# Conditioning vectors formed as columns by TensorE, their bias carried with the small vectors, context blocks rounded on ScalarE

## The chip, the core and the metric

The kernel runs on one core of a Trainium2 chip. The metric is device time in microseconds of one execution, median of several. Names used below: PE is TensorE's matrix multiplication (PEld its weight loads), DVE is VectorE, ACT is ScalarE, POOL is GpSimd, SP is SyncE, whose queue carries most DMA transfers.

A matrix product on TensorE has a stationary operand (the weights, loaded by a weight load; here up to 128 columns) and a moving operand that streams through (here up to 512 columns). Operands in plain float32 are taken in two passes, so that one product in the program shows as two weight loads and two MATMUL records in the trace. Operands of type float32r take one pass. A transpose is a product with the identity.

## What is computed

One layer of a trunk over 2048 latent tokens of width 1024, with a context prefix of 256 tokens. The part of the reference that the change touches is the conditioning ("ada") of both streams, and the modulated context:

```python
ada = jnp.einsum('bd,lde->lbe', jax.nn.silu(c), w_ada) + b_ada[:, None, :]
ada_c = jnp.einsum('d,lde->le', jax.nn.silu(c_ctx), w_ada) + b_ada
...
sh1, sc1, g1, sh2, sc2, g2 = (m[:, None, :] for m in jnp.split(ada[l], 6, axis=-1))
csh1, csc1, cg1, csh2, csc2, cg2 = jnp.split(ada_c[l], 6, axis=-1)
...
hc = modulate(rmsnorm(xc, norm_mix[l]), csh1, csc1)      # h * (1 + scale) + shift
logf_f, k_f, logf_b, k_b, vc = hgrn2_gates(hc @ w_in[l][:, :3 * w], lb_f, lb_b, first)
...
h = modulate(rmsnorm(x, norm_mix[l]), sh1, sc1)
o, _, _ = token_mixers(h @ w_in[l], ...)
x = x + g1 * (o @ w_out[l])
x = x + g2 * conv_ffn(modulate(rmsnorm(x, norm_ffn[l]), sh2, sc2), ...)
```

`w_ada` is 1024 x 6144. The first stage of the kernel needs its first 2048 columns: the shift (columns 0 to 1023) and the scale (1024 to 2047), for two vectors, c and c_ctx.

## The kernel before

Activations lie transposed in SBUF, features on the 128 partitions, so shift and scale are wanted as columns: `s1` and `a1`, each 128 partitions x 2 streams x 8 blocks, where `a1` holds (1 + scale) times the gain `norm_mix`. Every large product is made of three float32r products: each operand is split into a rounded part (`hi`, a cast on ScalarE) and the rest (`lo`, a subtraction on VectorE or GpSimd), and hi x hi, lo x hi and hi x lo are added in PSUM. In the trace the context's parts are `ch` and `cl`, those of a weight tile `whi` and `wlo`.

The stage that the change edits is written in an order of its own (`manual_schedule`): each engine runs its instructions in the order of the source. The first 2048 columns of `w_ada` come as four groups g of 512 columns, each in two halves q (four of the eight 128-row blocks of the contraction). Groups 0 and 1 are the shift, 2 and 3 the scale. The work on them:

- Groups 2, 0 and 3 go through TensorE in `ada_products`: the two silu vectors `cs2` (2 columns) are the weights, and a tile of `w_ada` streams as 512 moving columns. The result is two rows of 512. `ada_columns` adds the bias row on VectorE, transposes the rows in four pieces of 2 x 128, and `put_ada` writes them to `s1` or `a1`.
- Group 1 goes through VectorE: `ada_sums` multiplies each `w_ada` block by a scalar and adds it to `acc` (16 instructions, whose start value holds the bias row), and TensorE adds `acc` over the partitions by products with a vector of ones (8 products, bank `pz`).
- The small vectors (norm gains, biases of other parts) come by ScalarE's DMA queue as rows of one tile `vr`, and one transpose makes columns of them, `vec`.
- The context's 256 rows are normalised (`x_square`, `x_scale`) and transposed into four PSUM banks `pct`. `ctx_mod` modulates one block of 128 features (VectorE, line 232), rounds it (ScalarE, line 120) and subtracts (GpSimd for blocks 0 to 3, VectorE for 4 to 7, line 121).

The tiles of `w_in` come through a ring of three SBUF buffers, `raw`; the first two hold the context's rows until these have been transposed. `split_w` makes `whi` and `wlo` of one column tile of 128, into one of two slots. After the edited stage, Tile's scheduler decides each engine's order: twelve context column tiles of 24 products each (three per head), and beside them `x_start`, which squares, scales, transposes and modulates the first eight blocks of latent rows. From there on the large products of the input projection fill TensorE.

Of the kernel before, what the change touches and what calls it, by code (L numbers as in the profile page):

```python
# [9 lines left out]
F32 = mybir.dt.float32  # L10
# [4 lines left out]
ALU = mybir.AluOpType  # L15
# [57 lines left out]
def tile_trunk(ctx, tc, x, c, cx, c_ctx, w_ada, b_ada, norm_mix, norm_ffn, w_in, hg_norm, sgu_g, sgu_b,  # L73
# [104 lines left out]
    with es1:  # L178
# [13 lines left out]
        def bank(tag):  # L192
            return ps.tile([P, 512], F32, tag=tag, name=tag, bufs={"pj": 3, "sc": 2, "mi": 3}[tag])
# [46 lines left out]

        cc = pm.tile([P, 2, 8], F32, name="cc")
# [4 lines left out]
        wts, rows, pa, nxt = {}, {}, {}, {}  # L246
# [12 lines left out]
        def load_bias(g, tag):  # L259
            rows[g] = pm.tile([2, 512], F32, tag=tag, name="rows", bufs=2)  # L260
            ld(rows[g], b_ada[0:1, g * 512:(g + 1) * 512].broadcast_to([2, 512]))

        def ada_products(g, q):
            if q == 0:
                pa[g] = bank("pj")
            for k in range(4 * q, 4 * q + 4):
                T.matmul(pa[g][:2, :], cs2[:, k, :], wts[g, q][:, k % 4, :], start=(k == 0), stop=(k == 7))

        def ada_columns(g):
            V.tensor_add(rows[g], rows[g], pa.pop(g)[:2, :])  # L270
            pv = bank("pj")
            for j in range(4):
                T.transpose(pv[:, 2 * j:2 * j + 2], rows[g][:, j * P:(j + 1) * P], ident[:2, :2])
            put_ada(g, [pv[:, w:8:2] for w in range(2)])
# [7 lines left out]
        def put_ada(g, cols):  # L282
            sl = slice(4 * (g % 2), 4 * (g % 2) + 4)
            for w in range(2):
                if g < 2:
                    V.tensor_copy(s1[:, w, sl], cols[w])
                else:
                    V.scalar_tensor_tensor(out=a1[:, w, sl], in0=cols[w], scalar=1.0, in1=nmix[:, sl],
                                           op0=ALU.add, op1=ALU.mult)
# [4 lines left out]
        def ctx_mod(k, eng):  # L294
            x_mod(pct[k // 2][:, (k % 2) * 256:(k % 2) * 256 + 256], 1, k, chl[:, k, :], cll[:, k, :], CTX, eng)
# [4 lines left out]
        with tc.manual_schedule():  # L300
# [3 lines left out]
            vr = pm.tile([50, P], F32, tag="gu", name="vr", bufs=2)  # L304
            for a, n, r0 in ((norm_mix[0], 8, 0), (norm_ffn[0], 8, 8), (hg_norm[0], 4, 16), (sgu_g[0], 4, 20),
                             (sgu_b[0], 4, 24), (conv_b[0], 22, 28)):
                S.dma_start(vr[r0:r0 + n, :], a.rearrange("(r p) -> r p", p=P))
            load_bias(2, "ot")
# [3 lines left out]
            load_bias(0, "ot")  # L312
            for w in range(2):
                ld(acc[0:1, w, :], b_ada[0:1, 512:1024])
            load_bias(3, "vv")
            load_ada(3)
            load_raw((0, CTX))
            S.activation(sg, cc, AF.Sigmoid)
# [5 lines left out]
            T.transpose(pv[:, :50], vr, ident[:50, :50])  # L324
            V.tensor_copy(vec, pv[:, :50])
            ada_products(2, 1)
            ada_columns(2)
# [7 lines left out]
            load_raw((HW, CTX))  # L335
            ada_products(0, 1)
            ada_columns(0)
            ada_sums(4, 5)
            for k in range(4):
                ctx_mod(k, G)  # L340
                if k == 1:
                    ada_sums(5, 6)
            ada_products(3, 0)
# [3 lines left out]
            ada_sums(6, 8)  # L347
            nxt[0, CTX] = split_w((0, CTX), G)
# [6 lines left out]
            ada_columns(3)  # L355
            put_ada(1, [pz[:, 8 * w:8 * w + 8:2] for w in range(2)])
            for k in range(4, NK):
                ctx_mod(k, V)
            nxt[HW, CTX] = split_w((HW, CTX), V)
# [1349 lines left out]
```

## Time and profile before

| | us |
|---|---|
| median of 3 runs | 2528.61 |
| lowest and highest | 2525.8, 2529.62 |
| the profiled execution, its own time | 2527.3 |
| its span, first to last instruction | 2525.3 |

| engine | busy us | share of the span |
|---|---|---|
| PE | 2441.6 | 97% |
| PEld | 2016.9 | 80% |
| DVE | 1798.5 | 71% |
| POOL | 1059.3 | 42% |
| ACT | 957.6 | 38% |

How the lines are read. A line of the view in order of time gives the start, the duration, the engine, the line of the source, the operation, "out<-in" by the program's names, the shape, the count of instructions merged, and in brackets the idle time of the engine before it with what ended it. A line by stretches gives the stretch, its length, and for each engine named the busy time and the count; then the granted clock of TensorE (1.00 is full, 0.50 half), the DMA share and GB/s. A line of the view by groups gives line, engine, operation, names, shapes, count, then busy us and mean ns of one, then idle us before with what ended it. The recorded end of a MATMUL is modelled, and matmuls overlap, so their price is read from start to start.

### The profile page before, as it was taken

The numbers are of one execution on the slowest core, as the hardware profiler recorded it, in microseconds if no ns is written. First come the engines' busy times: TensorE is split into PE (matmuls) and PEld (weight loads), VectorE is DVE, ScalarE is ACT, GpSimd is POOL, SyncE is SP. The second block draws the span as 40 slices with busy tenths as digits, with TensorE's granted clock in tenths as the row PEclk, the third lists the DMA queues.
The fourth block names the chain that finished last, engine by engine and source line by source line (L and its number), as shares of the span: only waits on it lengthen the run. The fifth ranks groups of instructions, "written<-read, shape, count | busy, mean of one in ns | idle before, by whom it ended". The sixth has DMA issues, their size and how long they took to land.

```text
span 2525.3 us, 32815 instructions
## 1 busy us (share of the span) xinstructions
PE 2441.6 (97%) x11859; PEld 2016.9 (80%) x11859; DVE 1798.5 (71%) x2375; ACT 957.6 (38%) x1598; POOL 1059.3 (42%) x871
## 2 busy tenths in 40 slices
PE   7999999999999999899999999999999999999998
PEld 4787887888888888788778888878878887888886
DVE  5867884745756647465699778749999993676875
ACT  3553334434334343245433333324333342332352
POOL 1444232232233343100587787877778870000002
PEclk9999999999999999999999999999999999999999
DMA  8365436563353322668932222472222248843754
GB/s 292 101 196 171 143 116 199 183 241 117 117 180 127 115 84 101 225 210 251 306 104 83 95 79 88 147 260 85 81 91 85 96 134 332 280 150 128 235 160 149
DMA packets 305838, 400.13 MB, mean 158 GB/s; under 512 B 33025, under 2 KB 216057, under 8 KB 301965
## 3 DMA queue, kind: packets, MB, share of 16 engines
q1 hardware_dynamic: 302420, 397.30, 47.5%
q8 instruction: 94, 1.54, 0.2%
q10 hardware_dynamic: 3257, 0.75, 0.1%
q14 instruction: 67, 0.55, 0.1%
HBM read 288.85 MB, written 109.13 MB: 158 GB/s over the span
## 4 chain that ended last, share of the span: by engine, by line
PE 38%; DVE 7%; DMA 3%; issue 1%; POOL 1%; ACT 0%; SPq 0%; POOLq 0%; DVEq 0%; ACTq 0%
PE up L65 26%; PE dn L65 12%; DVE dn L1297 3%; DMA mr<-m 1%; DMA sT<-wd 1%; DVE edges L1302 1%; DVE mhl L121 0%; DMA raw<-in_w_up_dram 0%; POOL Al L121 0%; DVE gp L1373 0%; DMA yl<-yd 0%; DVE mr L1552 0%; DVE odd L1577 0%; DVE odd L1643 0%; POOL cv L1384 0%
## 5 line engine op out<-in xcount | busy, mean ns | idle before, releaser
L1297 DVE SCALAR_TENSOR_TENSOR dn<-gp,taps,dn 128x1024 f32<-128x1024 f32 x352 | 448.1, 1279 | 20.6 <-ACT dn L1294 17.4
L121 POOL TENSOR_TENSOR Al<-raw,Ah 128x512 fp32r<-128x512 f32 x264 | 344.6, 1313 | 97.5 <-ACT Ah L120 89.3
L65 PE MATMUL pj<-xh,whi 128*128 128x512 f32 x896 | 364.1, 407 | 0.5 <-ACT xh L120 0.5
L65 PE MATMUL pj<-xl,whi 128*128 128x512 f32 x896 | 351.3, 392 | 1.8 <-DVE xl L121 1.1
L65 PE MATMUL pj<-xh,wlo 128*128 128x512 f32 x896 | 351.5, 392 | 1.0 <-DVE wlo L121 1.0
L65 PE MATMUL dn<-th,mhl 128*128 128x512 f32 x1120 | 347.8, 392 | 3.1 <-ACT mhl L120 1.9
L65 PE MATMUL up<-xah,Al 128*128 128x512 f32 x704 | 277.0, 393 | 2.7 <-POOL Al L121 2.7
L65 PE MATMUL up<-xah,Ah 128*128 128x512 f32 x704 | 277.6, 394 | 1.9 <-ACT Ah L120 1.9
L65 PE MATMUL up<-yl,Ah 128*128 128x512 f32 x704 | 275.0, 391 | 2.6 <-DMA yl<-yd 2.6
L120 ACT CAST Ah<-raw 128x512 fp32r<-128x512 f32 x264 | 160.4, 618 | 292.9 <-PE up L65 241.8
L65 PEld LDWEIGHTS dn<-th,mhl 128*128 128x128 f32 x1120 | 211.0, 188 | 52.4 <-ACT mhl L120 2.3
L121 POOL TENSOR_TENSOR wlo<-raw,whi 128x1024 fp32r<-128x1024 f32 x56 | 142.2, 2539 | 217.7 <-ACT whi L120 185.5
L113 POOL TENSOR_SCALAR rs<-ss 128x2 f32<-128x2 f32 (+1 forms) x16 | 7.7, 480 | 534.2 <-ACT jk L1569 363.8
L65 PE MATMUL dn<-tl,mhl 128*128 128x512 f32 x560 | 221.5, 396 | 0.0
L65 PE MATMUL up<-yh,Ah 128*128 128x512 f32 x528 | 208.3, 395 | 0.0
L65 PE MATMUL up<-yh,Al 128*128 128x512 f32 x528 | 206.9, 392 | 0.0
L65 PE MATMUL up<-xal,Ah 128*128 128x512 f32 x528 | 206.3, 391 | 0.0
L65 PEld LDWEIGHTS pj<-xh,wlo 128*128 128x128 f32 x896 | 168.4, 188 | 37.0 <-DVE wlo L121 1.7
L65 PEld LDWEIGHTS pj<-xh,whi 128*128 128x128 f32 x896 | 169.0, 189 | 34.0 <-issue 3.5
L65 PEld LDWEIGHTS pj<-xl,whi 128*128 128x128 f32 x896 | 169.1, 189 | 33.1 <-DVE xl L121 2.1
L65 PE MATMUL dn<-wo,o 128*128 128x512 f32 x768 | 185.1, 397 | 3.7 <-DMA wo<-wo_d 2.2
L65 PEld LDWEIGHTS dn<-wo,o 128*128 128x128 f32 x768 | 143.0, 190 | 34.1 <-DMA wo<-wo_d 3.0
(321 smaller groups left out, 4662.2 us busy)
## 6 DMA issues: line engine op xcount, KB each, us to landing
raw<-in_w_up_dram SPq DMA_DIRECT2D x88, 512.0 KB
mr<-m SPq DMA_DIRECT2D x85, 512.0 KB
raw<-in_w_in_dram SPq DMA_DIRECT2D x68, 512.0 KB
sT<-wd SPq DMA_DIRECT2D x88, 256.0 KB
raw<-in_w_ada_dram SPq DMA_DIRECT2D x32, 512.0 KB
m<-cv SPq DMA_DIRECT2D x22, 544.0 KB
raw<-in_w_down_dram SPq DMA_DIRECT2D x22, 512.0 KB
wd<-raw SPq DMA_DIRECT2D x22, 512.0 KB
```

Of the source, the lines that this page charges most:

```text
L65: return self.engine.matmul(out, lhsT, rhs, **kw)
L113: keep(G.tensor_scalar(out=r[:, :n], in0=ss, scalar1=scale, scalar2=bias, op0=ALU.mult, op1=ALU.add))
L120: keep(S.copy(hi, raw))
L121: (eng or G).tensor_sub(lo, raw, hi.bitcast(F32))
L1297: V.scalar_tensor_tensor(out=cr, in0=gt[:, t // 3:t // 3 + RH, t % 3:t % 3 + GW], scalar=taps[:, t * NF + f:t * NF + f + 1], in1=cr, op0=A ...
L1302: V.scalar_tensor_tensor(out=e[:, 0, :], in0=gt[:, 1, t % 3:t % 3 + GW], scalar=taps[:, t * NF + f:t * NF + f + 1], in1=e[:, 0, :], op0=AL ...
```

## The change

- The two roles of the operands are exchanged in `ada_products`: tiles of `w_ada`, 128 x 128, are the weights, and the two columns of `cs2` stream. The result lies as columns in PSUM. Each half q of a group gives its own sum: 16 products (4 pieces of 128 columns, each over 4 blocks of the contraction), where there were 4. `put_ada` adds the two halves on VectorE.
- `load_bias`, the bias rows, `ada_columns` with its twelve small transposes, and the bias rows put into `acc` go. The 2048 bias values come as 16 more rows of `vr` (one more transfer on ScalarE's queue), and after the transpose they are copied to `bc`, with 1 added for the scale.
- `put_ada` handles both streams in one instruction of 128 x 2 x 4, with the gain multiplied in one more for the scale.
- `ctx_mod` has its own code. For blocks 0 to 3 ScalarE modulates and then rounds by a copy; for blocks 4 to 7 VectorE modulates while ScalarE modulates and rounds by itself, from PSUM. The subtraction is on VectorE for blocks 0 to 3, 4 and 6, on GpSimd for 5 and 7.
- `load_raw((HW, CTX))` is called earlier in the source; its transfer still waits until the context's rows have been transposed. Both first weight tiles are split ahead of the second half of group 3, on VectorE.
- The acc sums of group 1 stand in another place: ten before the shift of group 0, six behind it.

In the changed program's order on the engines, VectorE's addition for the first half of group 3 stands behind the six sums and the four subtractions of blocks 0 to 3, and the products of the second half of group 3 on TensorE wait for that addition. ScalarE's casts for the first two weight tiles follow block 3, and the cast for the fourth tile follows three of the four squares of the latent rows. SP's transfers of the second and third weight tile wait for the transposes of the context, with the latent rows behind them, as before. From about the 390th product of TensorE on, the order on the engines is that of the kernel before.

```diff
@@ -238,12 +238,13 @@
 
 
 
         cc = pm.tile([P, 2, 8], F32, name="cc")
         ld(cc[:, 0, :], c[0].rearrange("(p k) -> p k", k=8))
         ld(cc[:, 1, :], c_ctx.rearrange("(p k) -> p k", k=8))
         sg = pm.tile([P, 2, 8], F32, name="sg")
         wv = w_ada.rearrange("(p k) e -> p k e", k=8)
-        wts, rows, pa, nxt = {}, {}, {}, {}
+        wts, pa, nxt = {}, {}, {}
         pct = [bank("mi"), bank("mi"), bank("mi"), bank("sc")]
         xc = [raw_tile() for i in range(2)]
         acc = ph.tile([P, 2, 512], F32, tag="S", name="acc")
@@ -256,22 +257,15 @@
                 wts[g, q] = t.rearrange("p a (b e) -> p (a b) e", e=512)
                 ld(wts[g, q], wv[:, 4 * q:4 * q + 4, g * 512:(g + 1) * 512])
 
-        def load_bias(g, tag):
-            rows[g] = pm.tile([2, 512], F32, tag=tag, name="rows", bufs=2)
-            ld(rows[g], b_ada[0:1, g * 512:(g + 1) * 512].broadcast_to([2, 512]))
+        bc = pm.tile([P, 16], F32, name="bc")
 
         def ada_products(g, q):
             if q == 0:
                 pa[g] = bank("pj")
-            for k in range(4 * q, 4 * q + 4):
-                T.matmul(pa[g][:2, :], cs2[:, k, :], wts[g, q][:, k % 4, :], start=(k == 0), stop=(k == 7))
-        def ada_columns(g):
-            V.tensor_add(rows[g], rows[g], pa.pop(g)[:2, :])
-            pv = bank("pj")
             for j in range(4):
-                T.transpose(pv[:, 2 * j:2 * j + 2], rows[g][:, j * P:(j + 1) * P], ident[:2, :2])
-            put_ada(g, [pv[:, w:8:2] for w in range(2)])
+                for k in range(4):
+                    T.matmul(pa[g][:, 8 * q + 2 * j:8 * q + 2 * j + 2], wts[g, q][:, k, j * P:(j + 1) * P],
+                             cs2[:, 4 * q + k, :], start=(k == 0), stop=(k == 3))
 
         def ada_sums(k0, k1):
             for k in range(k0, k1):
@@ -279,20 +273,32 @@
                     V.scalar_tensor_tensor(out=acc[:, w, :], in0=wts[1, k // 4][:, k % 4, :], scalar=cs2[:, k, w:w + 1],
                                            in1=acc[:, w, :], op0=ALU.mult, op1=ALU.add)
 
-        def put_ada(g, cols):
+        def put_ada(g, cols, q):
             sl = slice(4 * (g % 2), 4 * (g % 2) + 4)
-            for w in range(2):
-                if g < 2:
-                    V.tensor_copy(s1[:, w, sl], cols[w])
-                else:
-                    V.scalar_tensor_tensor(out=a1[:, w, sl], in0=cols[w], scalar=1.0, in1=nmix[:, sl],
-                                           op0=ALU.add, op1=ALU.mult)
+            dst = (s1, a1)[g // 2][:, :, sl]
+            V.tensor_add(dst, cols, dst if q else view(bc, 4 * g, [[0, 2], [1, 4]]))
+            if g > 1 and q:
+                V.tensor_mul(dst, dst, view(vec, sl.start, [[0, 2], [1, 4]]))
+        def ada_put(g, q):
+            put_ada(g, pa[g][:, 8 * q:8 * q + 8].rearrange("p (j w) -> p w j", w=2), q)
 
         chl = pk.tile([P, NK, CTX], F32R, tag="F", name="ch", align_bytes=AL)
         cll = ph.tile([P, NK, CTX], F32R, tag="Q", name="cl", align_bytes=AL)
 
         def ctx_mod(k, eng):
-            x_mod(pct[k // 2][:, (k % 2) * 256:(k % 2) * 256 + 256], 1, k, chl[:, k, :], cll[:, k, :], CTX, eng)
+            pt = pct[k // 2][:, (k % 2) * 256:(k % 2) * 256 + 256]
+            sc, sh = a1[:, 1, k:k + 1], s1[:, 1, k:k + 1]
+            fl = pm.tile([P, 512], F32, tag="sig", name="xfl", bufs=2)
+            if k < 4:
+                S.activation(fl[:, :CTX], pt, AF.Identity, bias=sh, scale=sc)
+                S.copy(chl[:, k, :], fl[:, :CTX])
+            else:
+                V.tensor_scalar(out=fl[:, :CTX], in0=pt, scalar1=sc, scalar2=sh, op0=ALU.mult, op1=ALU.add)
+                S.activation(chl[:, k, :], pt, AF.Identity, bias=sh, scale=sc)
+            eng.tensor_sub(cll[:, k, :], fl[:, :CTX], chl[:, k, :].bitcast(F32))
 
         xg = [ph.tile([P, D], F32, tag=t, name="xg", bufs=2) for t in ("vt", "vt", "sgt", "sgt")]
         x_rows = [x[i * P:(i + 1) * P, :] for i in range(2 * NCH)]
@@ -301,30 +307,29 @@
             load_ada(2)
             for i in range(2):
                 ld(xc[i], cx[0][i * P:(i + 1) * P, :])
-            vr = pm.tile([50, P], F32, tag="gu", name="vr", bufs=2)
-            for a, n, r0 in ((norm_mix[0], 8, 0), (norm_ffn[0], 8, 8), (hg_norm[0], 4, 16), (sgu_g[0], 4, 20),
-                             (sgu_b[0], 4, 24), (conv_b[0], 22, 28)):
+            vr = pm.tile([66, P], F32, tag="gu", name="vr", bufs=2)
+            for a, n, r0 in ((norm_mix[0], 8, 0), (b_ada[0, 0:2 * D], 16, 50), (norm_ffn[0], 8, 8), (hg_norm[0], 4, 16),
+                             (sgu_g[0], 4, 20), (sgu_b[0], 4, 24), (conv_b[0], 22, 28)):
                 S.dma_start(vr[r0:r0 + n, :], a.rearrange("(r p) -> r p", p=P))
-            load_bias(2, "ot")
             for q in range(2):
                 load_ada(0, q)
                 load_ada(1, q)
-            load_bias(0, "ot")
-            for w in range(2):
-                ld(acc[0:1, w, :], b_ada[0:1, 512:1024])
-            load_bias(3, "vv")
             load_ada(3)
             load_raw((0, CTX))
+            load_raw((HW, CTX))
             S.activation(sg, cc, AF.Sigmoid)
             V.tensor_mul(cs2.rearrange("p k w -> p w k"), cc, sg)
             ss = x_sums()
             x_square(xc, ss, keep=lambda i: i)
             ada_products(2, 0)
             pv = bank("sc")
-            T.transpose(pv[:, :50], vr, ident[:50, :50])
+            T.transpose(pv[:, :66], vr, ident[:66, :66])
             V.tensor_copy(vec, pv[:, :50])
+            V.tensor_copy(bc[:, :8], pv[:, 50:58])
+            V.tensor_scalar(out=bc[:, 8:], in0=pv[:, 58:66], scalar1=1.0, scalar2=None, op0=ALU.add)
             ada_products(2, 1)
-            ada_columns(2)
+            for q in range(2):
+                ada_put(2, q)
             x_scale(xc, ss, keep=lambda i: i)
             ada_sums(0, 4)
             ada_products(0, 0)
@@ -332,31 +337,30 @@
                 for i in range(2):
                     o = (k % 2) * 256 + i * P
                     T.transpose(pct[k // 2][:, o:o + P], xc[i][:, k * P:(k + 1) * P], ident)
-            load_raw((HW, CTX))
             ada_products(0, 1)
-            ada_columns(0)
             ada_sums(4, 5)
+            for q in range(2):
+                ada_put(0, q)
+            ada_products(3, 0)
+            ada_sums(5, 8)
             for k in range(4):
-                ctx_mod(k, G)
-                if k == 1:
-                    ada_sums(5, 6)
-            ada_products(3, 0)
+                ctx_mod(k, V)
+            ada_put(3, 0)
             load_raw((2 * HW, CTX))
             for i in range(4):
                 ld(xg[i], x_rows[i])
-            ada_sums(6, 8)
-            nxt[0, CTX] = split_w((0, CTX), G)
+            for c in (0, HW):
+                nxt[c, CTX] = split_w((c, CTX), V)
             ada_products(3, 1)
             pz = bank("pj")
             for w in range(2):
                 for j in range(4):
                     o = 2 * (4 * w + j)
                     T.matmul(pz[:, o:o + 2], acc[:, w, j * P:(j + 1) * P], ones[:, :2], start=True, stop=True)
-            ada_columns(3)
-            put_ada(1, [pz[:, 8 * w:8 * w + 8:2] for w in range(2)])
+            ada_put(3, 1)
+            put_ada(1, pz[:, :16:2].rearrange("p (w j) -> p w j", w=2), 0)
             for k in range(4, NK):
-                ctx_mod(k, V)
-            nxt[HW, CTX] = split_w((HW, CTX), V)
+                ctx_mod(k, G if k % 2 else V)
         xl = p1.tile([P, NK, TH], F32R, tag="xl", name="xl", align_bytes=AL)
         xh = p1.tile([P, NK, TH], F32R, tag="xh", name="xh", align_bytes=AL)
 
```

## The prediction

> **What bounds the kernel now.** I read the page first, then the busy time by stage, then the order of time of the first 60 us. The chain of waits is followed back only to 1229 us, so it says nothing of the stage that is edited.
>
> ```profile
> PE 2441.6 (97%) x11859; PEld 2016.9 (80%) x11859; DVE 1798.5 (71%) x2375; ACT 957.6 (38%) x1598; POOL 1059.3 (42%) x871
> ```
>
> TensorE is busy for 97% of the span: a delay of its stream comes out nearly whole at the end. The stages (us, then busy time of PE, PEld, DVE, ACT, POOL, then granted clock):
>
> ```profile
> 30.00:40.00 10.00, 6.44 (x22) 1.87 (x20) 9.83 (x12) 2.57 (x5) 6.92 (x5) 1.00 1.05 377
> 60.00:70.00 10.00, 8.78 (x70) 8.25 (x71) 10.00 (x16) 5.49 (x11) 3.86 (x2) 1.00 0.49 142
> ```
>
> Between 30 and 40 us VectorE has 9.83 of 10 us: it, not TensorE, holds back the first context product. In order of time:
>
> ```profile
> 7.09 4.89 PE L65 MATMUL pj<-wa,cs 128*2 128x512 f32 x8 [7.09 <-DMA wa<-in_w_ada_dram]
> 11.91 0.26 PE L69 MATMUL sc<-ident,vr 50*128 50x50 f32 x1
> 12.10 3.60 PE L65 MATMUL pj<-wa,cs 128*2 128x512 f32 x8
> 17.06 1.41 DVE L227 TENSOR_SCALAR raw<-raw,rs 128x1024 f32<-128x1024 f32 x2
> 20.33 1.53 PE L69 MATMUL mi<-ident,raw 128*128 128x128 f32 x12
> 21.69 0.60 PE L69 MATMUL sc<-ident,raw 128*128 128x128 f32 x4
> 22.15 5.39 DVE L279 SCALAR_TENSOR_TENSOR acc<-wa,cs,acc 128x512 f32<-128x512 f32 x8 [3.69 <-DMA acc<-in_b_ada_dram]
> 22.22 3.60 PE L65 MATMUL pj<-wa,cs 128*2 128x512 f32 x8
> 33.96 5.71 DVE L279 SCALAR_TENSOR_TENSOR acc<-wa,cs,acc 128x512 f32<-128x512 f32 x4
> 39.10 2.32 PE L65 MATMUL pj<-ones,acc 128*128 128x2 f32 x16 [3.56 <-POOL wlo L121]
> 41.87 0.58 PE L65 MATMUL pj<-ch,whi 128*128 128x256 f32 x1
> ```
>
> Each half group of conditioning is 4 products, shown as 8 passes: 3.60 us, but 4.89 for the first, where the clock was still low. The acc sums start 3.69 us late, behind a bias row's transfer, and end at 39.67; the ones products follow, and the first context product starts at 41.87. That moment is what the change moves.
>
> **The passes that replace the products.** A half group becomes 16 products of 128 weight columns on 2 moving columns: 32 passes. The ones products have exactly this shape, with both clocks in their one burst (first row: weight loads):
>
> ```profile
> 39.07:40.40 1.33, 1.33 (x12) 1.00 0.87 313
> ...
> 40.64 0.35 PE L65 MATMUL pj<-ones,acc 128*128 128x2 f32 x1
> 40.86 0.35 PE L65 MATMUL pj<-ones,acc 128*128 128x2 f32 x1
> 41.07 0.35 PE L65 MATMUL pj<-ones,acc 128*128 128x2 f32 x1
> ```
>
> At clock 1.00 a pass costs 1.33/12 = 0.111 us, at 0.50 (41.07 - 40.64)/2 = 0.215. A half group is then 3.55 or 6.88 us, where it was 3.60. So the clock decides the sign:
>
> ```profile
> 6.33:9.74 3.41, 2.65 (x4) 0.50 (x5) 0.00 (x0) 0.00 (x0) 0.00 (x0) 1.00 1.05 411
> 37.05:40.46 3.41, 1.36 (x13) 1.39 (x13) 3.21 (x3) 0.00 (x0) 1.41 (x1) 1.00 0.97 376
> 40.46:43.87 3.41, 3.41 (x19) 3.38 (x19) 1.31 (x7) 0.40 (x1) 0.00 (x0) 0.50 1.02 343
> 43.87:47.29 3.42, 3.33 (x14) 2.72 (x12) 2.24 (x6) 1.01 (x3) 0.00 (x0) 0.50 0.23 87
> ...
> 40.46:41.86 1.40, 1.40 (x10) 0.50 0.97 255
> 41.86:43.87 2.01, 2.01 (x10) 0.50 1.05 405
> ```
>
> The clock changes only at steps of 3.41 us. The stretch 6.33 to 9.74 raised it with 2.65 us of streaming (its 1.00 is filled in, as no clock change precedes it: the passes ran at half speed). The stretch 40.46 to 43.87 had TensorE busy throughout and did not raise it (it stayed 0.50 to 47.29): 1.40 us of 2-column passes and 2.01 us of 256-column products. If a stretch is judged by a sum of its work, the bar lies above 2.01 and at or below 2.65 us of streaming, and 1.40 us of 2-column work counts for less than 0.64. A stretch full of it counts for less than 3.41 x 0.64 / 1.40 = 1.56, below a bar that 2.01 missed. So in the changed kernel, which starts cold and issues only such passes, I take 0.215 for all of them; the other end is 0.111. The Trainium skill, TensorE: Matmul & The Clock Gate, Part 1, says the same of the default (half rate until a busy window of about 3.4 us) and the trace agrees at 3.41; its word is "busy", and if weight loads were busy, rival C's time would follow.
>
> **The change part by part**, against the profiled execution (2527.3 us; span 2525.3).
>
> 1. TensorE's way to the first context product. It starts at 7.09 as before (the same transfers lead). Six half groups are 192 passes, the ones products 16: 208 x 0.215 = 44.7. The 16 transposes of the context took 1.89 us to 22.22; at half clock 3.8 (the rows for either end). The transpose of the small vectors 0.3 (0.26 before). The last half group writes the bank that VectorE's addition for the half group before it reads, so TensorE waits for that addition, behind VectorE's sums and subtractions; at half clock these are done by about 45 and it is a hop of 0.2 to 0.7, I take 0.5. Sum: 7.1 + 44.7 + 3.8 + 0.3 + 0.5 = 56.4, against 41.87: **+14.5**.
>
> 2. What is removed is hidden by this. Three bias additions, twelve transposes and five bias transfers go, the acc sums lose their 3.69 us wait, and four evictions leave VectorE; but with sums ending near 43, TensorE arrives at the ones products at 53. The bias in ScalarE's transfers adds one issue and 8 KB, due at 12 to 14 us: nothing. SP's queue loses five issues, but its second and third weight blocks wait for the transposes (now about 32), and the rows of x behind them; they are needed after 60.
>
> 3. The context blocks. Prices:
>
> ```profile
> L221 ACT ACTIVATE xjk<-xg 128x1024 bf16<-128x1024 f32 x4 | 4.2, 1060 | 0.0
> L121 POOL TENSOR_TENSOR cl<-xfl,ch 128x256 fp32r<-128x256 f32 x4 | 4.2, 1058 | 17.1 <-ACT ch L120 17.1
> L121 DVE TENSOR_TENSOR cl<-xfl,ch 128x256 fp32r<-128x256 f32 x4 | 1.7, 425 | 1.9 <-ACT ch L120 1.9
> L232 DVE TENSOR_SCALAR xfl<-mi,a,s 128x256 f32<-128x256 f32 x6 | 3.1, 538 | 0.3 <-POOL cl L121 0.2
> L514 ACT ACTIVATE cS<-pj 128x256 f32<-128x256 f32 x2 | 0.8, 380 | 0.2 <-issue 0.2
> ```
>
> Blocks 0 to 3 fall under TensorE's delay. Blocks 4 to 7 need the shift, which comes after the ones products: 0.3, then on VectorE 4 x 0.54 + 2 x 0.43 = 3.0, the last subtraction on GpSimd 1.06, its products 0.4: 4.8 us for the first column tile. ScalarE's rounding from PSUM (0.38, by its 128x256 activation) runs beside. Before:
>
> ```profile
> 48.22 0.28 PE L65 MATMUL pj<-ch,wlo 128*128 128x256 f32 x1
> 57.80 0.28 PE L65 MATMUL pj<-ch,wlo 128*128 128x256 f32 x1
> 57.92 0.28 PE L65 MATMUL pj<-ch,whi 128*128 128x256 f32 x1
> ...
> 53.88 1.05 ACT L120 CAST whi<-raw 128x1024 fp32r<-128x1024 f32 x1 [1.62 <-PE pj L65]
> ...
> 48.47 1.23 DVE L121 TENSOR_TENSOR wlo<-raw,whi 128x1024 fp32r<-128x1024 f32 x1 [0.52 <-ACT whi L120]
> 51.25 1.22 DVE L121 TENSOR_TENSOR wlo<-raw,whi 128x1024 fp32r<-128x1024 f32 x1 [1.55 <-ACT whi L120]
> 54.97 1.23 DVE L121 TENSOR_TENSOR wlo<-raw,whi 128x1024 fp32r<-128x1024 f32 x1 [2.49 <-ACT whi L120]
> 59.24 1.42 DVE L227 TENSOR_SCALAR xg<-xg,rs 128x1024 f32<-128x1024 f32 x2 [0.91 <-POOL rs L115]
> ...
> 64.47 0.21 DVE L477 TENSOR_TENSOR tot<-tot 128x64 f32<-128x64 f32 x1
> 66.34 0.42 DVE L470 TENSOR_TENSOR cS<-cS,tot 128x256 f32<-128x256 f32 x1
> ```
>
> 41.87 to 48.5 was 6.6: **-1.8**.
>
> 4. The second column tile. Its weight split moves ahead; it ran from 48.5 to 53.8 (the slot that the cast at 53.88 waited for), with a wait for wlo and a low clock; with neither, 24 products at the 0.12 between the rows at 57.80 and 57.92 are 2.9: **-2.4**.
>
> 5. Given back. In the changed order ScalarE's cast for the fourth tile stands behind the second tile's first sigmoid and three squares: 0.2 + 2 x 0.3 + 2 x 1.15 after the second tile ends, then 1.05 + 1.23 + 0.2 for the split: 5.6, against 2.9 of third tile: up to 2.7 of stall, or none if TensorE fills it. I take **+1.3**. VectorE is full from 60 to 70; of its scan updates two pairs of a total and an update (0.21 + 0.42 each) move ahead of the scaling of x: **-1.3**.
>
> Sum: 14.5 - 1.8 - 2.4 + 1.3 - 1.3 = **+10.3**: 2537.6. The shown runs' median, 2528.6, is 1.3 above the profiled one: **2539 us**.
>
> **Rivals.** *B: the transposes raise the clock.* 3.8 us of 128-column streaming could lift it for one step of 3.41 us, which does 6.6 us of cold passes: 3.2 less, 2536. For: they stream; against: they straddle two stretches. The Trainium skill, same page, Part 4, says that transposes do not count as busy in the same way; by it B falls and 2539 stands; no row here decides.
>
> *C, the other side: the clock rises as it did at 9.74 and 2-column passes keep it.* Then 12 passes cold to 9.74 and 20 x 0.111 to 12.0; four half groups, 14.2, transposes 1.9, vectors 0.2: 28.3; the wait of part 1 decides now: the 16 sums at 5.39/8 = 0.67 from about 17.6 (group 2 done at 15.7, its additions 0.5, the scaling 1.41) end at 28.7 with two additions, four subtractions 1.7, and the addition: 31. Then 3.55 + 16 x 0.111: 36.4, that is -5.5, and parts 3 to 5 unchanged: -9.7, **2519**. For: before stayed at 1.00 from 9.74 to 40.46. Against: it streamed 512 columns there, and the stretch 37.05 to 40.46, with 1.36 us of 2-column passes, lost the clock.
>
> *D: the delay is swallowed.* From 48.5 to 59.24 VectorE idles 5.5 us (0.52, 1.55, 2.49 and 0.91 ahead of its splits and scaling); if the x path used that, +4.8, 2533. Against: ScalarE's squares stand behind the late sigmoids in the order.
>
> **How the numbers follow.** Forecast 0.53, B 0.23, C 0.16, D 0.08. The forecast's own range is 2535 to 2543 (stall 0 to 2.7, hop and transposes 1 each way). Leaving out C and a little of each tail: 2527 to 2545. What this kernel's runs can tell from no change is about 0.2%, 5 us: slower holds the forecast and most of B, 0.73; within, the rest of B and D, 0.11; faster C, 0.16.
>
> **What would show it.** Right: 2-column passes 0.215 apart up to about 53 us, no raised clock before the context products, the first of these near 56. B: one raised step after the transposes. C: 0.111 apart and the first context product near 36. Wrong altogether: that product near 56 and an end within 5 us of before.

## The result and the profile after

The changed kernel ran in 2547.36 us (median of four: 2547.71, 2539.53, 2547.3, 2547.41), the kernel before beside it in 2527.2: slower by a ratio of 1.0072 [1.0057, 1.0087]. The profiled execution is the one of 2547.71 us, span 2545.6: **+20.3 us** over the profiled execution of before, where the sum had +10.3. The forecast's direction was right, its size half, and the time lies above the range. A second group of runs (six of the changed kernel, the first experiment below) puts the two medians 17.3 us apart, so the 20.3 of this pair may hold some of the spread of single executions.

The page's line of engines; TensorE is again busy for 97% of a longer span:

```profile
PE 2464.9 (97%) x11991; PEld 2057.8 (81%) x11991; DVE 1799.0 (71%) x2374; ACT 959.7 (38%) x1602; POOL 1048.6 (41%) x868
```

TensorE's first 57 us in order of time (start, duration, engine, line, operation, count, idle time before and what ended it):

```profile
7.25 6.96 PE L65 MATMUL pj<-cs,wa 128*128 128x2 f32 x32 [7.25 <-DMA wa<-in_w_ada_dram]
14.21 13.75 PE L65 MATMUL pj<-cs,wa 128*128 128x2 f32 x64
27.82 2.80 PE L69 MATMUL mi<-ident,raw 128*128 128x128 f32 x12
30.42 1.06 PE L69 MATMUL sc<-ident,raw 128*128 128x128 f32 x4
31.27 13.65 PE L65 MATMUL pj<-cs,wa 128*128 128x2 f32 x64
45.39 6.99 PE L65 MATMUL pj<-cs,wa 128*128 128x2 f32 x32 [0.47 <-DVE a L280]
52.24 3.55 PE L65 MATMUL pj<-ones,acc 128*128 128x2 f32 x16
55.66 0.56 PE L65 MATMUL pj<-ch,whi 128*128 128x256 f32 x1
```

The 32 passes of a half group take 6.81 us from start to start (7.25 to 14.06), 0.213 each, and those behind them the same (13.61 us for 64); the 16 transposes show one record each (12 and 4); the wait in front of the last half group is 0.47; the first context product starts at 55.66, 13.8 us later than before. The stages from 60 us on (us, then busy time of PE, PEld, DVE, ACT, POOL, then clock, which the view fills in with 1.00 up to the first recorded change; that change, a rise, is at 60.59):

```profile
60.00:70.00 10.00, 7.42 (x55) 6.81 (x54) 4.34 (x10) 7.03 (x14) 0.74 (x1) 1.00 0.18 53
70.00:80.00 10.00, 7.50 (x46) 6.84 (x46) 7.56 (x12) 3.83 (x7) 1.97 (x3) 0.83 0.50 158
90.00:100.00 10.00, 6.51 (x29) 4.87 (x28) 8.13 (x9) 4.58 (x10) 5.14 (x4) 0.91 0.22 66
```

TensorE is idle in 2.58, 2.50 and 3.49 of these 10 us. In order of time, the two places where it waits (the first block ScalarE's queue with TensorE and VectorE below it, the second GpSimd against VectorE):

```profile
63.54 1.05 ACT L120 CAST whi<-raw 128x1024 fp32r<-128x1024 f32 x1 [2.64 <-PE pj L65]
65.03 1.06 ACT L221 ACTIVATE xjk<-xg 128x1024 bf16<-128x1024 f32 x1
66.33 1.06 ACT L221 ACTIVATE xjk<-xg 128x1024 bf16<-128x1024 f32 x1
67.64 1.07 ACT L221 ACTIVATE xjk<-xg 128x1024 bf16<-128x1024 f32 x1
68.68 1.06 ACT L120 CAST whi<-raw 128x1024 fp32r<-128x1024 f32 x1
69.61 1.08 ACT L221 ACTIVATE xjk<-xg 128x1024 bf16<-128x1024 f32 x1
69.79 0.38 PE L65 MATMUL pj<-ch,whi 128*128 128x256 f32 x1 [1.00 <-ACT whi L120]
70.42 1.22 DVE L121 TENSOR_TENSOR wlo<-raw,whi 128x1024 fp32r<-128x1024 f32 x1
71.70 0.39 PE L65 MATMUL pj<-ch,wlo 128*128 128x256 f32 x1 [1.41 <-DVE wlo L121]
72.83 2.74 DVE L227 TENSOR_SCALAR xg<-xg,rs 128x1024 f32<-128x1024 f32 x4 [1.19 <-POOL rs L115]
...
93.71 0.52 POOL L113 TENSOR_SCALAR rs<-xss 128x4 f32<-128x4 f32 x1
95.29 2.34 POOL L121 TENSOR_TENSOR wlo<-raw,whi 128x1024 fp32r<-128x1024 f32 x1
95.36 4.81 DVE L227 TENSOR_SCALAR xk<-xk,rs 128x1024 f32<-128x1024 f32 x4 [1.18 <-POOL rs L115]
98.32 0.45 PE L69 MATMUL mi<-ident,xk 128*128 128x128 f32 x1 [3.31 <-DVE xk L227]
125.31 0.35 DVE L450 SCALAR_TENSOR_TENSOR rh<-mi,vec,bsb 128x128 f32<-128x128 f32 x1 [0.25 <-PE mi L65]
```

First place: both early tiles end together, ScalarE's cast for the third starts at 63.54 (the corresponding release of before stands at 53.88, 9.7 earlier), and from there ScalarE has no gap until 72.0: three of the four squares stand between this cast and the next one at 68.68, the fourth behind it, and TensorE waits for the fourth tile's cast (1.00) and for its remainder (1.41), which VectorE begins at 70.42, 0.68 after that cast's end. x is scaled at 72.83, 13.6 us later than before. Second place: GpSimd begins the one weight subtraction it does here 0.07 us ahead of VectorE's scaling of xk; the scaling takes 4.81 us where four take 2.74, and TensorE waits 3.31 for it. Before, that subtraction and xk looked like this:

```profile
75.16 2.39 POOL L121 TENSOR_TENSOR wlo<-raw,whi 128x1024 fp32r<-128x1024 f32 x1
75.96 2.08 DVE L470 TENSOR_TENSOR cf<-cf 128x256 f32<-128x256 f32 x1
79.14 0.52 POOL L113 TENSOR_SCALAR rs<-xss 128x4 f32<-128x4 f32 x1
81.96 2.74 DVE L227 TENSOR_SCALAR xk<-xk,rs 128x1024 f32<-128x1024 f32 x4
106.10 0.60 DVE L446 SCALAR_TENSOR_TENSOR rh<-mi,vec,bsb 128x128 f32<-128x128 f32 x2
```

It ran before xk's root (rs, the factor by which the rows are normalised; 75.16 against 79.14), beside an update of cf; after, it stands behind the root (95.29 against 93.71), and so beside the scaling.

The first operation on VectorE that writes rh (a later stage; line 446 before, 450 after) is the mark used below: from the first context product to it the kernel before takes 64.2 us (106.10 - 41.87), the changed one 69.7 (125.31 - 55.66). At rh the changed kernel is 19.2 us late, and 1.1 more at the end.

### The profile page after: what moved, and what is told of

Its sections match the earlier page's. It is cut to its first block, busy times and chain, and to the rows that moved or that the text cites. A ratio compares the mean times of both kernels' runs of the same rounds, so it can differ in the third digit from the quotient of the medians.

```text
span 2545.6 us, 33071 instructions
## 1 busy us (share of the span) xinstructions
PE 2464.9 (97%) x11991; PEld 2057.8 (81%) x11991; DVE 1799.0 (71%) x2374; ACT 959.7 (38%) x1602; POOL 1048.6 (41%) x868
## 5 line engine op out<-in xcount | busy, mean ns | idle before, releaser
L1301 DVE SCALAR_TENSOR_TENSOR dn<-gp,taps,dn 128x1024 f32<-128x1024 f32 x352 | 448.4, 1280 | 20.6 <-ACT dn L1298 17.3
```

The lines of the kernel that those rows point to most:

```text
L1301: V.scalar_tensor_tensor(out=cr, in0=gt[:, t // 3:t // 3 + RH, t % 3:t % 3 + GW], scalar=taps[:, t * NF + f:t * NF + f + 1], in1=cr, op0=A ...
```

## The experiments

First product and distance are read from each run's profile (kernel before: 41.87 and 64.2); the ratio is to the kernel before, run on the same chip. Single times of one kernel spread by up to 16 us there (before: 2519.18 to 2535.3 in one group of 32), so the positions in the traces say more than a median.

| run | first context product, us | distance to rh, us | median, us | before, us | ratio |
|---|---|---|---|---|---|
| changed kernel again | 55.48 | 69.2 | 2542.20 | 2524.95 | 1.0065 [1.0049, 1.008] |
| delay in the old order | 56.29 | 64.3 | 2538.78 | 2524.95 | 1.0048 [1.0033, 1.0063] |
| rows | 37.38 | 67.4 | 2522.30 | 2524.95 | 0.9987 [0.9977, 0.9998] |
| warm start | 51.88 | 69.7 | 2542.34 | 2524.95 | 1.0058 [1.0038, 1.0078] |
| eighth split on VectorE | 55.34 | 64.6 | 2541.46 | 2528.61 | 1.0047 [1.0029, 1.0065] |
| second split back | 55.45 | 68.9 | 2544.78 | 2528.61 | 1.0058 [1.0038, 1.0077] |
| rounding alone | 39.97 | 63.7 | 2525.85 | 2528.61 | 0.999 [0.9976, 1.0003] |
| columns alone | 52.02 | 71.4 | 2544.02 | 2528.61 | 1.0052 [1.0032, 1.0073] |
| eighth split, squares early | 52.29 | 58.3 | 2530.42 | 2526.42 | 1.002 [1.0008, 1.0032] |
| rows, eighth split | 35.90 | 64.4 | 2517.29 | 2526.42 | 0.9966 [0.9955, 0.9977] |
| rows, eighth split, squares early | 43.68 | 61.8 | 2524.28 | 2526.42 | 0.9999 [0.9987, 1.0011] |
| before, eighth split on VectorE | 43.04 | 64.2 | 2526.37 | 2526.42 | 1.0003 [0.999, 1.0016] |

**The changed kernel again.** No edit.

> The changed kernel once more, unaltered, as the measure for the other runs. Its profiled execution reached the first context product at 55.66 us (41.87 before, 13.8 later), scaled x at 72.83 (59.24 before, 13.6 later) and ended 20.3 us later. Theory: the 13.8 us come from conditioning passes at the half clock, and the other 6 to 7 are stalls of TensorE between 60 and 115 us that the new order brings, such as the 3.31 us ahead of the transposes at 98.32. If these stalls belong to the order, they come back in every execution: a time of 2545 to 2548. Rival: they hang on where the 3.41 us steps of the clock happen to fall; then the times spread, with several near the 2539.5 that one of four runs had.

Measured: the wait of 3.31 us stands in this execution too, xk is scaled in 4.81 again, the distance is 69.2, although its clock lost a further step, at 66.6 us. So the stalls belong to the order. The six times (2537.01 to 2546.54) spread more than that theory had it: one of them lies between 2545 and 2548.

**A pure delay.** In the kernel before:

```diff
             pz = bank("pj")
+            for i in range(48):
+                T.matmul(pz[:, 16:18], ident, cs2[:, 0, :], start=True, stop=True)
```

> The kernel before with 48 products of two columns (the identity on the activated conditioning) ahead of the ones products, into columns that nobody reads; everything else in the old order. It delays the first context product by TensorE work alone, to 53 to 62 us from 41.87. Theory (the extra 6 to 7 us of the changed kernel come from its order): the end moves by as much as the first context product does or by a little less, 11 to 15 us for a product at 55, with no growth behind it. Rival (a delay of this kind grows by itself behind the first context product): the end moves by some 6 us more than that product.

Measured: the first product moves by 14.4 us, and the distance is 64.3 as before: in the trace x and xk are scaled 14.5 us late and rh starts 14.5 us late, no more and no less. Up to rh, then, a delay does not grow by itself, and none of it is swallowed either (rival D). The medians lie 13.8 apart. The traced execution itself ended only 6.9 us behind the profiled one of before (spans 2532.2 and 2525.3): behind rh single executions differ by that much, and one pair of them says little there.

**Rows again.** In the changed kernel:

```diff
...
+            for k in range(4 * q, 4 * q + 4):
+                T.matmul(pa[g][:2, :], cs2[:, k, :], wts[g, q][:, k % 4, :], start=(k == 0), stop=(k == 7))
+        def ada_columns(g):
+            row = pm.tile([2, 512], F32, tag="ot", name="row", bufs=2)
+            S.copy(row, pa[g][:2, :])
+            pv = bank("pj")
             for j in range(4):
-                for k in range(4):
-                    T.matmul(pa[g][:, 8 * q + 2 * j:8 * q + 2 * j + 2], wts[g, q][:, k, j * P:(j + 1) * P],
-                             cs2[:, 4 * q + k, :], start=(k == 0), stop=(k == 3))
+                T.transpose(pv[:, 2 * j:2 * j + 2], row[:, j * P:(j + 1) * P], ident[:2, :2])
+            put_ada(g, pv[:, :8].rearrange("p (j w) -> p w j", w=2), 0)
...
```

> The changed kernel with the conditioning products as rows again (512 columns stream, the row is copied by ScalarE and turned by four transposes), bias and context rounding as in the changed kernel, and nearly its order. Theory: the loss of 13.8 us is the half clock under the two-column passes; with rows the clock rises at 9.74 us as before, the first context product stands near 35 to 40 us and the end 2 to 10 us earlier than the kernel before if the order behind it costs nothing, and near the time before if the order costs its 6 to 7 us here too. Rival: something else of the change (the sums, the additions of bias, the weights' arrival) holds the first context product; then it stays above 45 us and the time above 2535.

Measured: 37.38 us, 18.1 earlier than with columns, with all else of the change in place. The clock is raised at 12.61 here. Against the kernel before the product is 4.5 us earlier, but the distance, 67.4, is 3.2 longer (the scaling of xk takes 4.81 here too), and the time is 2.6 us under it.

**A warm start.** In the changed kernel, ahead of the first half group:

```diff
+            warm = bank("pj")
+            for i in range(20):
+                T.matmul(warm[:, :P], ones, ones, start=True, stop=True)
             ada_products(2, 0)
```

> The changed kernel with 20 products of 128 columns (ones on ones) ahead of the first half group, in the 7 us in which TensorE has nothing to do. It tells what two-column passes do to a clock that is already raised. Theory (such passes neither raise the clock nor hold it, as the stretch 40.46 to 43.87 of the kernel before suggests): the clock is raised by 7 to 10 us and lost one or two steps of 3.41 us after the passes begin; they run at 0.111 us for a few us only, the first context product comes 3 to 6 us earlier than 55.66. Rival (the passes hold a raised clock, they only can't raise it): 0.111 us throughout, first context product at 36 to 39 us, and a time near or below the time before.

Measured, TensorE in order of time:

```profile
1.12 6.45 PE L65 MATMUL pj<-ones 128*128 128x128 f32 x40 [1.12 <-POOL ones L90]
7.40 3.63 PE L65 MATMUL pj<-cs,wa 128*128 128x2 f32 x32
10.90 0.25 PE L69 MATMUL sc<-ident,vr 66*128 66x66 f32 x1
10.99 13.21 PE L65 MATMUL pj<-cs,wa 128*128 128x2 f32 x64
```

and by the stretches of the clock (columns as above):

```profile
4.75:8.16 3.41, 3.41 (x33) 3.41 (x32) 0.18 (x1) 0.20 (x1) 0.00 (x0) 1.00 1.00 363
8.16:11.58 3.42, 3.42 (x33) 3.42 (x32) 0.35 (x3) 0.00 (x0) 0.00 (x0) 1.00 1.03 382
11.58:14.99 3.41, 3.41 (x18) 3.41 (x17) 0.00 (x0) 2.30 (x4) 0.51 (x2) 0.50 1.05 401
```

The streams raise the clock, the first 32 passes run in 3.50 us (7.40 to 10.90, 0.109 each), and after the stretch 8.16 to 11.58, filled with such passes and one transpose, the clock is at 0.50 again. So two-column passes do not hold a raised clock here, and rival C could not have come about even with the clock raised at the start. The first product comes 3.6 us earlier; with the distance at 69.7 the median shows nothing of that.

**The eighth weight split on VectorE.** In the changed kernel:

```diff
-            split(hi, lo, raw, eng or (V if w_n[0] < 8 or w_n[0] < 20 and w_n[0] % 2 else G))
+            split(hi, lo, raw, eng or (V if w_n[0] < 9 or w_n[0] < 20 and w_n[0] % 2 else G))
```

> The changed kernel with the eighth weight split subtracted on VectorE and not on GpSimd. In the changed kernel that subtraction (2.34 us on GpSimd at 94.91) runs beside the scaling of xk on VectorE, which takes 4.81 us for four where the kernel before took 2.74, and TensorE waits 3.31 us for it. Measure: the distance from the first context product to the first rh operation on VectorE, 64.2 us before, 69.2 and 69.7 in the two executions of the changed kernel. Theory (the two engines hold each other up there): the scaling takes 2.74 again, that wait falls to about 1 us, the distance to 67 to 67.5 and the end by 2 us. Rival (the scaling is late because the squares and the root ahead of it are, and GpSimd's work is beside the point): the wait stays over 2.5 us and the distance within 0.7 us of 69.5.

Measured:

```profile
94.89 2.74 DVE L227 TENSOR_SCALAR xk<-xk,rs 128x1024 f32<-128x1024 f32 x4 [1.18 <-POOL rs L115]
95.79 0.30 PE L69 MATMUL mi<-ident,xk 128*128 128x128 f32 x1 [1.23 <-DVE xk L227]
119.92 0.35 DVE L450 SCALAR_TENSOR_TENSOR rh<-mi,vec,bsb 128x128 f32<-128x128 f32 x1 [0.19 <-PE mi L65]
```

The wait for the root stays (1.18), the scaling is back at 2.74, TensorE's wait at 1.23, and the distance at 64.6: the whole growth is gone, 4.6 to 5.1 us for the place of one subtraction. The medians do not show it by themselves: the intervals of the two ratios overlap. The expected 2 us were too few. The traces tell something of the rest: from the scaling of xk to rh it is 25.0 us here, 30.0 and 29.7 in the two executions of the changed kernel, where TensorE's clock lost a step behind its wait (98.13 to 101.55 in the first), and 28.0 in the next run, which has the collision but kept its clock at 1.00 there. So about 3 us would go with the collision and its wait and 2 with the lost step; the orders differ, and this was not tested by itself.

**The second split back behind the blocks.** In the changed kernel:

```diff
-            for c in (0, HW):
-                nxt[c, CTX] = split_w((c, CTX), V)
+            nxt[0, CTX] = split_w((0, CTX), V)
...
                 ctx_mod(k, G if k % 2 else V)
+            nxt[HW, CTX] = split_w((HW, CTX), V)
```

> The changed kernel with the split of the second tile's weights put back behind the context blocks. Theory A (taking both weight slots early is what makes the third and fourth tile wait for their casts and shifts the later work): the distance from the first context product to the first rh operation falls from 69.5 towards 64.2 us, to 66 or less, and the end comes 3 to 5 us earlier than the changed kernel's 2542. Theory B (the extra stalls come from the planner's order of the later work, which any edit of this stage rearranges): the distance stays at 68 to 71 and the time within 2 us.

Measured: 68.9, so theory A falls. Theory B's distance is met (its time, 2544.78, is 2.6 us from 2542, on another chip). What stands behind the number is the same collision: GpSimd's subtraction starts at 96.33, the scaling of xk at 96.39 and takes 4.82, in another order.

**Rounding alone.** The kernel before with the new `ctx_mod` (its first blocks' subtraction on VectorE, the last on both engines).

> The kernel before with only the new rounding of the context blocks (ScalarE's activation from PSUM). The prediction's step 3 gave it about 1.8 us on the first context tile together with the share between GpSimd and VectorE. Theory: the first column tile ends 0.5 to 2 us earlier than before, the conditioning is untouched (first context product 41 to 42 us), distance from there to the first rh operation 63 to 65 us, and the time within 2 us of before. Rival (the rearranged order costs here too): the distance grows by 2 us or more to over 66, and the time is 2526 to 2530 or more.

Measured: the first product 1.9 us earlier than before, although the clock was raised later (12.23 against 9.74), the distance 0.5 us shorter, the time not told apart from before. This part costs nothing. On a like clock it gains more: the last run below has the order of before up to that product and its clock raised at 12.14, and reaches it at 43.04, 3.1 us later than here.

**Columns alone.** The kernel before with the new `ada_products`, `put_ada` and the bias rows in `vr`.

> The kernel before with only the columns and the bias in the small vectors' transfer; blocks and splits in the old place of the source. Theory: the passes at 0.215 us put the first context product at 53 to 57 us, as in the changed kernel (55.5), and the end follows by 12 to 16 us if the later order stays as before (distance to the first rh operation 64 to 65 us), by 17 to 20 if that order is rearranged to the worse (distance over 68). Rival (the late product is owed to the moved blocks and splits): it comes before 50 us.

Measured: first product at 52.02, distance 71.4 with the scaling of xk at 4.84 us beside the same subtraction. The slowdown is that of the columns, 15.4 us in the medians. The product is 3.5 us earlier than in the changed kernel, and the reason is rival B:

```profile
27.93 2.80 PE L69 MATMUL mi<-ident,raw 128*128 128x128 f32 x12
30.53 1.06 PE L69 MATMUL sc<-ident,raw 128*128 128x128 f32 x4
31.38 4.78 PE L65 MATMUL pj<-cs,wa 128*128 128x2 f32 x37
```

```profile
28.30:31.72 3.42, 3.42 (x19) 3.42 (x17) 0.21 (x1) 0.00 (x0) 0.00 (x0) 1.00 0.32 96
31.72:35.13 3.41, 3.41 (x32) 3.41 (x32) 0.00 (x0) 0.00 (x0) 0.00 (x0) 1.00 0.78 216
```

First TensorE in order of time, then its stretches (the first 1.00 is filled in, the rise is at 31.72): that from 28.30 to 31.72 holds 3.08 us of transposes (the next pass starts at 31.38), and the one after it has 32 passes, where 0.215 makes 16.

**The squares early.** On top of the eighth split on VectorE:

```diff
+            ssg = x_sums()
+            x_square(xg, ssg, keep=lambda i: i)
+            x_scale(xg, ssg, keep=lambda i: i)
             for c in (0, HW):
                 nxt[c, CTX] = split_w((c, CTX), V)
...
             for q in range(2):
-                x_square(xg[2 * q:2 * q + 2], ss, 2 * q)
...
-                if q:
-                    x_scale(xg, ss)
                 yield 2.0
```

> The changed kernel with the eighth weight subtraction on VectorE, and with the squares, the root and the scaling of xg moved ahead of the second half of the context blocks, into the time in which ScalarE waits 9.98 us for the shift. In the changed kernel TensorE ends the second column tile 9.7 us later than before and x is scaled 13.6 us later. Theory (the 4 us between the two are ScalarE's queue: four squares of 1.06 us and three weight casts of 1.05 us, all behind the sigmoids of tiles that now end together): without the squares there, the casts of the third and fourth tile come earlier, x is ready before it is wanted, and the distance from the first context product to the first rh operation falls from 64.6 us (eighth subtraction on VectorE alone) to 60 to 62. Rival (the 4 us are TensorE's, waiting for the two weight slots that come free together): the distance stays within 1 us of 64.6.

Measured:

```profile
60.44 1.05 ACT L120 CAST whi<-raw 128x1024 fp32r<-128x1024 f32 x1 [2.24 <-PE pj L65]
62.46 1.07 ACT L120 CAST whi<-raw 128x1024 fp32r<-128x1024 f32 x1
110.55 0.35 DVE L450 SCALAR_TENSOR_TENSOR rh<-mi,vec,bsb 128x128 f32<-128x128 f32 x1 [0.19 <-PE mi L65]
```

```profile
27.13:30.54 3.41, 3.41 (x17) 3.41 (x18) 2.34 (x4) 0.00 (x0) 0.00 (x0) 1.00 0.55 173
30.54:33.96 3.42, 3.42 (x34) 3.42 (x32) 0.00 (x0) 0.00 (x0) 0.00 (x0) 1.00 0.55 162
```

The two casts (third and fourth tile) stand 2.0 us apart instead of 5.1, and the distance is 58.3: 6.3 us less than with the eighth split alone, and more than expected. The rival falls; squares, root and scaling were moved together, so their shares are not told apart. Here too the transposes (from 27.57 on) raised one step of the clock, as the second block's 34 passes in one stretch show, and the first product came 3.1 us earlier; that part of the time is chance.

**Rows with the eighth split on VectorE.**

> Conditioning as rows with the rest of the change, and the eighth weight subtraction on VectorE. With rows alone the first context product stood at 37.38 us and the first rh operation 67.4 later; the subtraction on VectorE took 4.6 us from that distance in the changed kernel. Theory (the two effects are separate and add): first context product at 37 to 38, distance 63 to 64, and a time 4 to 5 us under that of rows alone, some 6 to 8 under the kernel before. Rival: the gain is used up behind it, and the time is within 2 us of rows alone (2.6 under the kernel before).

Measured: 35.90 and 64.4, the distance 3.1 us shorter than with rows alone; 9.1 us under the kernel before, the fastest of all and faster than both kernels: the change without its columns, and without the collision. It is a little more than expected; the first product is 1.5 us earlier than with rows alone because the clock was raised at 9.64 and not at 12.61 (the first half group took 4.90 us against 6.38), which the edit does not touch, and rh stands 5.9 us earlier than before, so some 3 of the 9.1 lie behind it, unexplained.

**Rows, eighth split, squares early.**

> The two former edits together: rows, eighth subtraction on VectorE, x squared and scaled early. Theory (ScalarE's queue): the distance falls by a further 2 to 4 us, the time to 8 to 12 us under the kernel before. Rival (weight slots): no further gain; or with TensorE 14 us earlier than in the changed kernel x has not landed in time, ScalarE's casts wait behind its squares, and the first context product moves to over 40 us.

Measured: the distance falls further, to 61.8, but the rival's second half came true: the first product moves to 43.68, and the time is that of the kernel before. ScalarE's squares wait for the rows of xg (1.11, 0.17 and 0.63 us for their transfers), and behind the squares stand the first two weight casts and the copy of the last conditioning row, for which TensorE waits 6.64 us. VectorE stands 7.65 us for the root of xg, and the shift for the later blocks stands behind that.

```profile
42.25 2.74 DVE L227 TENSOR_SCALAR xg<-xg,rs 128x1024 f32<-128x1024 f32 x4 [7.65 <-POOL rs L115]
43.16 0.59 PE L69 MATMUL pj<-ident,row 2*128 2x2 f32 x4 [6.64 <-ACT row L270]
43.68 0.58 PE L65 MATMUL pj<-ch,whi 128*128 128x256 f32 x1
```

What was idle time of ScalarE and VectorE under slow columns is not idle under rows.

**The kernel before with its eighth split on VectorE.**

> The kernel before with the eighth weight subtraction on VectorE. There that subtraction ran on GpSimd at 75.16 us beside an update of cf on VectorE, which took 2.08 us where the same shape on cS took 0.64. Theory (the price of that subtraction depends on what it meets, and the change moved it from an update to the scaling of xk): removing it gains 0 to 2 us in the kernel before where it gained 5 in the changed one; distance from the first context product to the first rh operation 62 to 64.2 us. Rival (it costs about 5 us wherever it falls): distance under 61.

Measured: distance 64.2, ratio 1.0003. The update of cf takes 0.61 us without the subtraction beside it (2.08 with it), and nothing waited for those 1.5 us. The collision was there before the change; it lay where nobody waited.

## Why the prediction was right in direction and wrong in size

The main term held. What failed is step 5, which was mis-sized, and a term of the same size that the sum did not have (6).

1. *TensorE's way to the first context product, +14.5*: +13.8 in the profiled execution, and the steps nearly as priced: passes 0.213 apart (0.215), hop 0.47 (0.5), transposes 3.45 (27.82 to 31.27; 3.8). The argument on the clock, that a stretch of such passes does not raise it, held, and more than was argued: the warm start shows that they lose a raised clock too. Rows in place of columns take 18.1 us off that product: the cause is shown.
2. *Removed work hidden*: from its start to 55.66 TensorE waits for nothing but the 0.47. Right.
3. *and* 4. *First and second column tile, -1.8 and -2.4*: from the first product's +13.8 to the release of the slot at +9.7 it is -4.1. Right in sum; the two were not told apart, as the tiles run interleaved.
5. *Given back, +1.3 and -1.3*: **this is the step that failed.** The stall was seen (the cast behind squares), but its sum of 5.6 us from the second tile's end to the fourth tile's remainder counts two of the three squares that it names and leaves out the third tile's cast, which now waits for the same end. The trace has 8.1 (63.54 to 71.64). The difference was then cut to half its upper bound of 2.7, and the squares were not followed on to the scaling of x, which waits for all four of them. It measures +3.9 (from +9.7 at the slot to +13.6 at the scaling of xg). With squares, root and scaling of xg out of the way the distance falls by 6.3. And the -1.3 for updates of the scan is not to be seen: with the eighth split on VectorE, scaling of xg to rh takes 47.6 us (119.92 - 72.33), against 46.9 before.
6. *Not in the sum at all*: the collision of GpSimd's subtraction with the scaling of xk. From the scaling of xg to rh the changed kernel takes 52.5 us and 47.6 without the collision: +4.9, the lost step of the clock included.

So 13.8 - 4.1 + 3.9 + 5.6 (4.9 collision, 0.7 others) + 1.1 behind rh = 20.3. The 1.1 has no cause shown; the two executions of the changed kernel differ by 2.8 there. The prediction followed the order up to the scaling of x and stopped; Tile's scheduler had also moved the root of xk ahead of the weight subtraction, on GpSimd's queue, 40 us behind the first context product.

**The rivals.** B had its mechanism right and its condition open: the transposes raise the clock when enough of them fall into one stretch. It took 2.97 us (27.57 to 30.54) and 3.08 us of them in two runs; 2.05 us in the changed kernel's first execution (27.82 to 29.87) and 2.27 us in the warm start (25.23 to 27.50) did not do it. The gain is the 3.2 us that was worked out (55.48 to 52.29 with the squares early). Which of the two comes is decided by where the steps fall. The Trainium skill, TensorE: Matmul & The Clock Gate, Part 4, has it that transposes do not engage the full clock; these two runs differ, and the measurement decides. C falls by the warm start, D by the pure delay.

## What to carry to other kernels

A product with few moving columns is not paid by those columns: at the low clock a pass with 2 of them took 0.213 us, a transpose with 128 took 0.216 (3.45 over 16), and the weight loads filled the stretches as much as the products did. A run of such passes costs half at the raised clock (0.109) but did not keep it raised. Put them where the clock is not needed, or stream the long side. After pricing an edit, follow the order of each queue as far as the next stages that share its engines; here the second largest term arose 40 us behind the edited stage, between two engines that the edit hardly touched. Work that blocks another engine is free only as long as nobody waits for what it blocks: the same subtraction cost nothing before the change and some 5 us after it.

## What was not expected of the hardware

GpSimd and VectorE hold each other up for the length of an instruction, not by a share: 4.81 us for a scaling that takes 2.74, 2.07 more, with a GpSimd subtraction of 2.34 us that began 0.07 us earlier. All of it is in the first of the four instructions (2.82 us; 0.74 for the next). It was 4.82 and 4.84 in the two other orders in which they met, and 2.74 or 2.75 in the runs in which they did not meet. The other way round, GpSimd's subtraction of 128x512 takes 3.38 at 64.57 in the kernel before, beside VectorE's, where 1.28 to 1.30 is usual. The Trainium skill, SBUF — State Buffer, section "Who interferes with whom", states such a lock: GpSimd and a VectorE instruction of certain kinds share one pair of ports, the first to start has it for its whole instruction, the other waits. The traces agree.

The busy time of TensorE's records is not what the clock goes by: stretches of 3.41 us filled with two-column passes (3.41 of 3.41 us busy) neither raised it, in 48 us of the changed kernel up to the first context product, nor held it in the warm start.
